# Hybrid attention and SSM layer: the input projection as seven half-size block products (Strassen), one product at a time

## Chip, cores and metric

The kernel runs on one core of a Trainium2 chip. The metric is the time of one execution in microseconds (us), measured on the device. The profile is of one execution, and all its rows are in us from the first instruction unless they say ns.

## What is computed

One layer over 2048 tokens of width 2048, all in float32. The input projection is the largest product: 2048 x 2048 by 2048 x 4608.

```python
h = rms_norm(x, norm_w)
proj = jnp.einsum('bld,de->ble', h, w_in)          # IN_W = 1024 + 256 + 256 + 1024 + 1024 + 1024
q, k, v, z_attn, u, z_ssm = jnp.split(proj, splits, axis=-1)
o_attn = swa_sink_attention(q, k, v, positions, q_norm_w, k_norm_w, sinks)   # window 128, 16 heads, 4 kv heads
o_attn = o_attn * jax.nn.silu(z_attn)
y = s5_ssm(u, a_re, a_im, log_step, b_re, b_im, c_re, c_im, d_skip)          # 64 groups of 16 channels
y = jax.nn.gelu(y)
y = y * jax.nn.sigmoid(y @ w_glu + b_glu)
o_ssm = y * jax.nn.silu(z_ssm)
merged = concat([rms_norm(o_attn, attn_out_norm_w), rms_norm(o_ssm, ssm_out_norm_w)])
out = x + jnp.einsum('ble,ed->bld', merged, w_out)
```

## The kernel before

Every large product is made of three passes in the fp32r type: each operand is split into a high part (a ScalarE cast) and a low part (a VectorE subtraction), and high x high, high x low and low x high are added up in PSUM.

**Tokens and panels.** The tokens are taken in two halves of 1024. For one half the whole normed and transposed x lies in SBUF, as 16 chunks of [128 features, 1024 tokens], each split into `xh` and `xl`. For the first half `x_first` (L242) loads rows of x, norms them and transposes them on TensorE; for the second half `x_stats` (L273) and `x_later` (L286) do so later, beside other work. The weight comes in units (`w_unit`, L304): a load of 256 KB, a cast `wh<-wr`, a subtraction `wl<-wr,wh`. A panel of u or z (`panel_feat`, L315) is 128 features by 1024 tokens: 16 chunks x 3 passes x 2 = 96 matmuls of 512 columns. A panel of q, k or v (`panel_tok`, L331) is 1024 tokens by 256 features with x as the weight operand: 16 x 8 x 3 = 384 matmuls of 256 columns. Over both halves there are 48 panels of the first kind and 12 of the second in the projection, 4608 matmuls of each kind.

**PSUM.** Four single banks (`psg`, [128, 512]) serve the panels, four more (`psa`) the small chains.

**What leaves a panel.** u, z, q, k and v go to DRAM scratch (`US`, `ZA`, `ZS`, `QS`, `KK`, `VS`). q and k are token-major: rotary and the norm of each head work along the free dimension (`rope_two`, L393), and `attend_in` (L467) transposes q on TensorE and splits it (`qst`).

**Order.** `run` (L1026) weaves panels with side work in steps (`weave`, L995): the SSM's tables (`ssm_setup`, L574) beside the first half's u, q, k, v and z; the first half's attention (`attend`, L503) beside the second half's start; the SSM itself (`ssm_pairs`, L784, 32 pairs) beside the rest of the projection. This stretch, up to about 1870 us, is called the front below. Then comes the tail: GLU of the first half (`glu`, L916) beside `tail_attn` (L885), the output projection of the first half (`out_panel`, L949) beside the second half's attention, GLU of the second half, and its output projection (`out_wide`, L970). The order of instructions within an engine is set by the tile framework, which schedules by a simulated timeline.

**Queues.** All loads and stores of tiles are issued from SyncE (SP), in one order. Staging tiles of 4 KB per partition come from one pool, `stg`, of 4 buffers; weight units from `wp` with 3 buffers each of raw, high and low.

```python
def tt(self, out, a, b, op, eng=None):      # nearly all two-input VectorE work is put down to this line, L84
    (eng or self.nc.vector).tensor_tensor(out=out, in0=a, in1=b, op=op)
```

## Time and profile before

| | |
|---|---|
| time, three runs | 2890.61 to 2895.2 us, median 2894.02 us |
| span of the profiled execution | 2892.7 us, the only time that it has |
| TensorE, matmuls | busy 2813.6 us (97%), 17123 instructions |
| TensorE, weight loads | 2515.5 us (87%) |
| VectorE | 1900.9 us (66%) |
| ScalarE | 968.2 us (33%) |
| GpSimd | 201.0 us (7%) |
| DMA | 369.09 MB, 128 GB/s over the span |

Busy time is the time in which an engine has at least one instruction under way; matmuls overlap one another, so that the duration of one is longer than the step from one to the next. VectorE's instructions overlap a little too. The span is the stretch from the first to the last instruction; it is 1.3 us under the median of the runs.

### The profile page before, as it was taken

What the parts mean: (1) busy time and instruction counts of PE and PEld (TensorE: products, weight loads), DVE (VectorE), ACT (ScalarE), POOL (GpSimd) and SP (SyncE); (2) the same over time, 40 slices, a digit from 0 to 9 for tenths busy, and PEclk for the clock granted to TensorE, in tenths of its full rate; (3) what the DMA queues carried; (4) which work ended last, traced back from release to release, by engine and by line L of the source; (5) the groups of instructions that cost most, each with busy time, mean ns of one, the idle gap of its engine ahead of it and who ended that gap; (6) DMA issues with size and microseconds to landing.
All of it is one profiled execution on the core that took longest, in us unless ns stands there. A gap on an engine that the chain in (4) does not pass through costs nothing.

```text
span 2892.7 us, 45678 instructions
## 1 busy us (share of the span) xinstructions
PE 2813.6 (97%) x17123; PEld 2515.5 (87%) x17123; DVE 1900.9 (66%) x4479; ACT 968.2 (33%) x2117; POOL 201.0 (7%) x341
## 2 busy tenths in 40 slices
PE   6899999989999999999999999998999999899999
PEld 5789999878888888888999988878999999778887
DVE  6681746856773776677779985378999875842222
ACT  6421212133442444333323332255444433521110
POOL 0000000001110021100000000000222220000000
PEclk9999999999999999999999999999999999999999
DMA  5842526553332533445455554343444436333321
GB/s 175 226 123 63 164 88 172 142 141 106 99 113 76 177 108 97 128 145 146 146 160 151 149 154 141 116 125 95 144 135 124 125 111 189 99 101 107 106 78 58
DMA packets 430541, 369.09 MB, mean 128 GB/s; under 512 B 56560, under 2 KB 388848, under 8 KB 430320
## 3 DMA queue, kind: packets, MB, share of 16 engines
q1 hardware_dynamic: 428256, 366.16, 42.6%
q8 instruction: 135, 2.21, 0.3%
q14 instruction: 86, 0.70, 0.1%
q10 hardware_dynamic: 2064, 0.01, 0.0%
HBM read 270.74 MB, written 99.55 MB: 128 GB/s over the span
## 4 chain that ended last, share of the span: by engine, by line
PE 81%; DVE 8%; DMA 7%; SPq 2%; ACT 1%; issue 1%; POOL 0%; ACTq 0%; POOLq 0%; DVEq 0%
PE psg L325 32%; PE psg L343 28%; PE psg L979 6%; PE pss L979 3%; DMA oa<-OA 2%; PE pss L516 2%; PE pso L556 2%; PE pso L979 1%; PE pst L979 1%; DVE ml L93 1%; DMA xst<-in_x_dram 1%; DVE yg L84 1%; PE pst L541 1%; DMA TCS<-St 1%; PE pss L810 1%
## 5 line engine op out<-in xcount | busy, mean ns | idle before, releaser
L84 DVE TENSOR_TENSOR wl<-wr,wh 128x512 fp32r<-128x512 f32 x456 | 315.4, 692 | 544.2 <-ACT wh L311 534.7
L311 ACT CAST wh<-wr 128x512 fp32r<-128x512 f32 x456 | 283.2, 622 | 1007.8 <-PE psg L325 330.9
L325 PE MATMUL psg<-xh,wl 128*128 128x512 f32 x1536 | 495.0, 394 | 7.2 <-DVE wl L84 7.2
L325 PE MATMUL psg<-xl,wh 128*128 128x512 f32 x1536 | 498.4, 395 | 0.0
L325 PE MATMUL psg<-xh,wh 128*128 128x512 f32 x1536 | 493.9, 395 | 0.5 <-ACT xh L235 0.5
L343 PE MATMUL psg<-wl,xh 128*128 128x256 f32 x1536 | 435.2, 284 | 0.0
L343 PE MATMUL psg<-wh,xh 128*128 128x256 f32 x1536 | 434.2, 284 | 1.0 <-ACT rx L389 1.0
L343 PE MATMUL psg<-wh,xl 128*128 128x256 f32 x1536 | 434.2, 284 | 0.0
L325 PEld LDWEIGHTS psg<-xh,wl 128*128 128x128 f32 x1536 | 287.8, 189 | 65.2 <-DVE wl L84 8.9
L325 PEld LDWEIGHTS psg<-xh,wh 128*128 128x128 f32 x1536 | 287.0, 189 | 57.2 <-ACT xh L235 0.9
L325 PEld LDWEIGHTS psg<-xl,wh 128*128 128x128 f32 x1536 | 288.1, 189 | 55.8
L343 PE MATMUL psg<-wh,mh 128*128 128x256 f32 x1024 | 289.9, 286 | 8.6 <-ACT tt L927 7.8
L343 PEld LDWEIGHTS psg<-wh,xh 128*128 128x128 f32 x1536 | 293.6, 192 | 1.4 <-ACT rx L389 1.2
L343 PEld LDWEIGHTS psg<-wl,xh 128*128 128x128 f32 x1536 | 294.2, 192 | 0.4 <-DVE wl L84 0.2
L343 PEld LDWEIGHTS psg<-wh,xl 128*128 128x128 f32 x1536 | 293.7, 192 | 0.0
L343 PE MATMUL psg<-wl,mh 128*128 128x256 f32 x1024 | 290.2, 285 | 0.6 <-DVE wl L84 0.6
L343 PE MATMUL psg<-wh,ml 128*128 128x256 f32 x1024 | 288.9, 285 | 0.0
L84 POOL TENSOR_TENSOR pm<-ph,sel 128x256 fp32r<-128x256 f32 x240 | 189.5, 811 | 983.1 <-ACT ph L544 647.2
L343 PEld LDWEIGHTS psg<-wh,mh 128*128 128x128 f32 x1024 | 195.1, 192 | 9.4 <-ACT tt L927 8.0
L343 PEld LDWEIGHTS psg<-wl,mh 128*128 128x128 f32 x1024 | 196.4, 192 | 0.8 <-DVE wl L84 0.8
L343 PEld LDWEIGHTS psg<-wh,ml 128*128 128x128 f32 x1024 | 195.4, 192 | 0.0
L533 ACT ACTIVATE sm<-pss,mx,rs 128x128 f32<-128x128 f32 x240 | 108.6, 459 | 96.3 <-DVE mx L93 90.5
(419 smaller groups left out, 4663.0 us busy)
## 6 DMA issues: line engine op xcount, KB each, us to landing
wr<-in_w_in_dram SPq DMA_DIRECT2D x296, 256.0 KB
wr<-in_w_out_dram SPq DMA_DIRECT2D x128, 256.0 KB
tb<-TCS SPq DMA_DIRECT2D x64, 256.0 KB
xr<-in_x_dram SPq DMA_DIRECT2D x64, 256.0 KB
out_dram<-xr SPq DMA_DIRECT2D x64, 256.0 KB
raw<-MBC SPq DMA_DIRECT2D x32, 384.0 KB
kst<-KK SPq DMA_DIRECT2D x56, 192.0 KB
xst<-in_x_dram SPq DMA_DIRECT2D x16, 512.0 KB
```

Of the source, the lines that this page charges most:

```text
L84: (eng or self.nc.vector).tensor_tensor(out=out, in0=a, in1=b, op=op)
L93: self.nc.vector.scalar_tensor_tensor(out=out, in0=a, scalar=s, in1=b, op0=op0, op1=op1)
L311: nc.scalar.copy(hi, raw)
L325: nc.tensor.matmul(ps[t], wt[:, kk, :], xx[k][:, t * 512:(t + 1) * 512], start=(k == 0 and i == 0), stop=(k == nkc - 1 and i == 2))
L343: nc.tensor.matmul(o, xx[k][:, sl], wt[:, kk, :], start=(k == 0 and i == 0 and t % 2 == 0), stop=(k == nkc - 1 and i == 2), skip_group_che ...
L516: nc.tensor.matmul(ps[:, h * 256:h * 256 + 256], qst[:, bq % 2, hp * 2 + h, :], kst[:, i, ksl], start=(h == 0 and i == 0), stop=(i == 1), ...
L533: nc.scalar.activation(sm[:, h, :], sc[:, h, :], AF.Exp, scale=rs[:, h:h + 1], bias=negm[:, h:h + 1], accum_out=den[:, h:h + 1])
L541: nc.tensor.transpose(pt[:, h * P:(h + 1) * P], sm[:, h, :], self.ident)
L556: nc.tensor.matmul(po, vst[:, blk + kb, :], pm[:, i, kb], start=(i == 0 and kb == 0), stop=(i == 1 and kb == 1))
L810: nc.tensor.matmul(o, m[:, g, 0:128], u[:, g, 384:640], start=(g == 0 and i == 0), stop=(i == 2), skip_group_check=True)
L979: nc.tensor.matmul(ps[t], xx[k0 + k][:, t * P:(t + 1) * P], wt[:, 0, :], start=(k == 0 and j == 0), stop=(k == 7 and j == 2))
```

## The change

The projection is computed for all 2048 tokens at once, as a 2 x 2 block product: tokens in halves, the 2048 inputs in halves, the output features in halves (paired as `fh` = 0, 1). Strassen's scheme in Winograd's form replaces the eight half-size products by seven. It is done in two groups: 10 pairs of panels (q, k, v, u) and 8 pairs (z_attn with z_ssm). In each group the products p = 0 to 6 run one after the other; a product is 10 or 8 panels, each of 8 chunks x 3 passes x 2 = 48 matmuls of 512 columns.

- **Left factors** (`form`, `place`). The host hands in x transposed as well (`xT`). The blocks and the four sums of blocks are formed once, 8 chunks of [128, 1024] each, stored to `AF` in DRAM, and loaded again for later products. x is still read row-wise for the norms (`x_stats`), and the factor of each token is spread over the partitions (`spread`, `rbc`).
- **Right factors** (`right`). The host lays the weight out as 4 KB runs per partition (`wl`). For p = 2, 5 and 6 the factor is a difference of two or three blocks, formed per panel; two of them are kept in `TW`.
- **Sums of products** (`gather`). Each panel's PSUM (a pair of banks, two such pairs) is added to a partial sum loaded from `CS` in DRAM, and the result is stored to `CS` or is an output.
- **q and k** are feature-major: `rope` works on [128 = 4 heads x 32, 1024 tokens] with both halves of each head; the first half to arrive waits in `RAW`. q is stored split (`QH`), so `attend_in` loads it ready with four DMAs, and k with four.
- z_attn is multiplied in `tail_attn` in place of `attend`.
- Staging: 7 buffers in the front and 4 in the tail; of x's split chunks 13 slots. The GLU weight is one load per panel (`wg`), the output weight comes in units of 512 KB.

```diff
-        self.wp = ep(tc.tile_pool(name="wp", bufs=3))
-        self.stg = ep(tc.tile_pool(name="stg", bufs=4))
-        self.gp = ep(tc.tile_pool(name="gp", bufs=4, space=PSUM))
+        self.gp = ep(tc.tile_pool(name="gp", bufs=2, space=PSUM))
...
+        return self.gp.tile([P, 1024], F32, tag="g", name="psg")
...
+    def norm_block(self, th, kh, k):
+        x = self.stage("xn")
+        r0 = kh * HT + k * P
+        self.ld.dma_start(x, self.a["xT"][r0:r0 + P, th * HT:(th + 1) * HT])
+        self.stt(x, x, self.nw[:, kh * 8 + k:kh * 8 + k + 1], self.rbc[th], ALU.mult, ALU.mult)
+        return x
...
+    def form(self, seq, k, first):
+        g = self.nc.gpsimd
+        p = seq % 7
+        st = lambda j, x: self.st.dma_start(self.AF[j, k], x)
+        if not first or p in (3, 4, 5, 6):
+            x = self.af_load(p, k)
+        elif p < 2:
+            x = self.norm_block(0, p, k)
+            st(p, x)
+        else:
+            n21 = self.norm_block(1, 0, k)
+            n22 = self.norm_block(1, 1, k)
+            st(6, n22)
+            s1 = self.stage("s1")
+            self.tt(s1, n21, n22, ALU.add)
+            st(3, s1)
+            x = self.af_load(0, k)
+            self.tt(n21, x, n21, ALU.subtract, g)
+            st(5, n21)
+            self.tt(x, s1, x, ALU.subtract)
+            st(2, x)
+            n12 = self.af_load(1, k)
+            self.tt(n12, n12, x, ALU.subtract, g)
+            st(4, n12)
+        return x
+
+    def place(self, seq, k, x):
+        slot = (8 * seq + k) % self.nslot
+        hi = self.xt.tile([P, HT], F32R, tag=f"xh{slot}", name=f"xh{slot}")
+        lo = self.xt.tile([P, HT], F32R, tag=f"xl{slot}", name=f"xl{slot}")
+        self.nc.scalar.copy(hi, x)
+        self.tt(lo, x, hi.bitcast(F32), ALU.subtract)
+        self.fac[seq % 2][k] = (hi, lo)
...
+        if p == 2:
+            b11, b12 = W(0, q1), W(0, q2)
+            self.tt(b12, b12, b11, ALU.subtract, g)
+            self.st.dma_start(self.TW[0, tw], b12)
+            b22 = W(1, q2)
+            self.tt(b22, b22, b12, ALU.subtract)
+            self.st.dma_start(self.TW[1, tw], b22)
+            return b22
+        if p == 3:
+            return self.w_load(self.TW[0, tw])
...
+        if p == 5:
+            b22, b12 = W(1, q2), W(0, q2)
+            self.tt(b22, b22, b12, ALU.subtract, g)
+            return b22
+        t2, b21 = self.w_load(self.TW[1, tw]), W(1, q1)
+        self.tt(t2, t2, b21, ALU.subtract, g)
+        return t2
+
+    def product(self, seq, group, first):
+        p = seq % 7
+        base, n = ((0, 10), (20, 8))[group]
+        free = self.nslot - 8
+        for i in range(n):
+            hi, lo = self.w_split(self.right(p, base + i, base + n + i))
+            ps = self.psg()
+            for k in range(8):
+                xh, xl = self.fac[seq % 2][k]
+                for j, (wt, xx) in enumerate(((hi, xh), (hi, xl), (lo, xh))):
+                    for t in range(2):
+                        nc.tensor.matmul(ps[:, t * 512:(t + 1) * 512], wt[:, k * P:(k + 1) * P], xx[:, t * 512:(t + 1) * 512],
+                                         start=(k == 0 and j == 0), stop=(k == 7 and j == 2))
+            if seq < 13 and i < free:
+                self.place(seq + 1, i, self.form(seq + 1, i, seq < 6))
+            if seq < 13 and i == n - 1:
+                for k in range(free, 8):
+                    self.place(seq + 1, k, self.form(seq + 1, k, seq < 6))
+            self.gather(p, group, i, ps)
+            yield
...
+        if p == 0:
+            t = self.stage("c0")
+            self.nc.scalar.copy(v(t), pv)
+            self.st.dma_start(cs(0), t)
+        elif p == 1:
+            done(0, 0, i, plus(load(0)))
+        elif p == 2:
+            self.st.dma_start(cs(1), plus(load(0)))
+        elif p == 3:
+            self.st.dma_start(cs(2), plus(load(1)))
+        elif p == 4:
+            done(0, 1, i, plus(load(2)))
+        elif p == 5:
+            b = load(1)
+            a = load(2)
+            self.st.dma_start(cs(3), plus(b))
+            done(1, 1, i, plus(a))
+        else:
+            done(1, 0, i, plus(load(3), ALU.subtract))
...
+            m, n = f2("rm"), f2("rn")
+            sh = (P, 2, 512)
+            self.stt(m, bc(a[:, s].unsqueeze(1), sh), wa, cs, ALU.mult, ALU.mult)
+            self.stt(n, bc(b[:, s].unsqueeze(1), sh), wb, cs, ALU.mult, ALU.mult)
+            self.tt(a[:, s], m[:, 0], n[:, 1], ALU.subtract)
+            self.tt(b[:, s], n[:, 0], m[:, 1], ALU.add)
...
+            self.x_stats(0)
+            for k in range(8):
+                self.place(0, k, self.form(0, k, True))
+            self.consts()
+            self.weave(pr(0, 2), self.setup_early(), 2, 0.0, 0.3, PU)
+        self.weave(pr(2, 5), self.ssm_setup(), 28, 0.0, 0.95, PU)
+        self.weave(pr(5, 14), self.mixers(), 65, 0.0, 1.0, PA)
+        phase.close()
```

## Rows read from the trace of the kernel before

**Rows 1.** The page, part 1: busy time, share and instructions of each engine.
```profile
PE 2813.6 (97%) x17123; PEld 2515.5 (87%) x17123; DVE 1900.9 (66%) x4479; ACT 968.2 (33%) x2117; POOL 201.0 (7%) x341
```

**Rows 2.** Tile yh: the first GLU matmul, that is the end of the front.
```profile
L325 PE MATMUL psg<-yh,wh x256: 387/389/632, 1870.3 to 2522.0; 128*128 128x512 f32 x128
```

**Rows 3.** Windows, front and tail: length, engines' busy us, granted clock, DMA share, GB/s.
```profile
0.00:1870.00 1870.00, 1822.52 (x10978) 1621.54 (x10979) 1260.98 (x3019) 619.94 (x1325) 99.60 (x213) 0.99 0.46 134
1870.00:2893.00 1023.00, 991.10 (x6147) 893.92 (x6145) 639.91 (x1460) 348.28 (x792) 101.36 (x128) 0.99 0.38 116
```

**Rows 4.** Groups of instructions on TensorE: one of three passes of each kind.
```profile
L325 PE MATMUL psg<-xh,wh 128*128 128x512 f32 x1536 | 493.9, 395 | 0.5 <-ACT xh L235 0.5
...
L343 PE MATMUL psg<-wh,xh 128*128 128x256 f32 x1536 | 434.2, 284 | 1.0 <-ACT rx L389 1.0
```

**Rows 5.** Chain that ended last: start, length, what; unbroken runs of matmuls.
```profile
1785.89 78.71 PE psg L325 x347
...
2373.85 52.56 PE psg L343 x438
```

**Rows 6.** SP's own waits: total us, times, longest.
```profile
SPq L308 <- DVE wl L84: 972.4, 288, 10.7
```

**Rows 7.** Timeline of TensorE: four transposes and the next matmul's start.
```profile
300.38 0.60 PE L733 MATMUL pst<-ident,BT 128*128 128x128 f32 x4
300.74 0.37 PE L343 MATMUL psg<-wh,xl 128*128 128x256 f32 x1
```

**Rows 8.** Timeline of VectorE: starts of neighbours in unbroken runs.
```profile
477.31 1.22 DVE L84 TENSOR_TENSOR tu<-St,us 128x1024 f32<-128x1024 f32 x1
478.45 1.22 DVE L84 TENSOR_TENSOR tv<-Ct,us 128x1024 f32<-128x1024 f32 x1
...
508.09 0.69 DVE L84 TENSOR_TENSOR tu<-St,us 128x512 f32<-128x512 f32 x1
508.69 0.69 DVE L84 TENSOR_TENSOR tv<-Ct,us 128x512 f32<-128x512 f32 x1
```

**Rows 9.** Groups of instructions on VectorE that the projection issues.
```profile
L84 DVE TENSOR_TENSOR wl<-wr,wh 128x512 fp32r<-128x512 f32 x456 | 315.4, 692 | 544.2 <-ACT wh L311 534.7 <-DMA wr<-in_w_in_dram 3.8 <-PE psg L325 2.5
...
L84 DVE TENSOR_TENSOR rtmp<-rx,rt 128x512 f32<-128x512 f32 x40 | 25.8, 686 | 0.0
```

**Rows 10.** Windows of three stretches: opening, end of GLU, output projection with attention.
```profile
0.00:100.00 100.00, 77.55 (x381) 63.29 (x382) 67.60 (x195) 56.64 (x97) 4.79 (x52) 1.00 0.58 178
...
1930.00:1985.00 55.00, 44.31 (x215) 37.80 (x214) 47.10 (x61) 32.95 (x42) 0.00 (x0) 0.88 0.25 79
...
1985.00:2373.00 388.00, 387.17 (x3261) 386.45 (x3260) 346.77 (x1054) 165.52 (x535) 101.36 (x128) 1.00 0.42 127
```

**Rows 11.** DMA issues: transfers and KB of each.
```profile
wr<-in_w_in_dram SPq DMA_DIRECT2D x296, 256.0 KB
...
xst<-in_x_dram SPq DMA_DIRECT2D x16, 512.0 KB
...
QS<-rx SPq DMA_DIRECT2D x16, 512.0 KB
```

**Rows 12.** Windows of 5 us with busy DMA engines, columns as in rows 3.
```profile
20.00:25.00 5.00, 1.11 (x4) 0.71 (x4) 4.38 (x22) 3.59 (x7) 0.00 (x0) 1.00 1.02 412
...
110.00:115.00 5.00, 4.65 (x21) 3.52 (x19) 5.00 (x9) 3.04 (x7) 0.00 (x0) 1.00 1.00 361
...
135.00:140.00 5.00, 4.74 (x21) 3.58 (x20) 4.83 (x33) 1.39 (x3) 0.00 (x0) 1.00 1.08 87
```

**Rows 13.** Tile pm, GpSimd and VectorE: duration ns min/median/max.
```profile
L84 POOL TENSOR_TENSOR pm<-ph,sel x240: 731/745/1248, 642.5 to 2367.7; 128x256 fp32r<-128x256 f32 x120
L84 DVE TENSOR_TENSOR pm<-pl,sel x240: 408/421/1021, 644.6 to 2368.0; 128x256 fp32r<-128x256 f32 x120
```

More of the change, by code (lines that the diff above doesn't have):

```diff
@@ new lines, in panel_glu @@
+    def panel_glu(self, m, xh, xl, evac):
+        nc = self.nc
+        ps = self.psg()
+        hi, lo = self.w_split(self.w_load(self.a["wg"][m]))
+        for k in range(8):
+            for i, (wt, xx) in enumerate(((hi, xh), (hi, xl), (lo, xh))):
+                for t in range(2):
+                    nc.tensor.matmul(ps[:, t * 512:(t + 1) * 512], wt[:, k * P:(k + 1) * P], xx[k][:, t * 512:(t + 1) * 512],
+                                     start=(k == 0 and i == 0), stop=(k == 7 and i == 2))
+        yield
+        for t in range(2):
+            evac(t, ps[:, t * 512:(t + 1) * 512])
@@ new lines, in run @@
+        with tc.tile_pool(name="rb", bufs=1) as pool:
+            self.rbc = [pool.tile([P, HT], F32, tag=f"rbc{h}", name=f"rbc{h}") for h in range(2)]
+            self.x_stats(0)
+            for k in range(8):
+                self.place(0, k, self.form(0, k, True))
[3 more added lines that the diff above has]
+        self.weave(pr(5, 14), self.mixers(), 65, 0.0, 1.0, PA)
@@ L1112, with laid_out @@
 _OUTS = [((1, 2048, 2048), "float32")]
+def laid_out(inputs):
+    o = {k: np.asarray(v) for k, v in inputs.items()}
+    o["xT"] = np.ascontiguousarray(o["x"][0].T)
+    half = lambda c0, two, i: [c0 + (i * 4 + h) * 64 + two * 32 + j for h in range(4) for j in range(32)]
+    run = lambda c0, m: list(range(c0 + m * P, c0 + m * P + P))
+    f = lambda two: ([half(C_Q, two, i) for i in range(4)] + [half(C_K, two, 0), run(C_V, two)]
+                     + [run(C_U, m + 4 * two) for m in range(4)])
+    panels = f(0) + f(1) + [run(C_ZA, m) for m in range(8)] + [run(C_ZS, m) for m in range(8)]
+    w = o["w_in"].reshape(2, 8, P, -1)
+    o["wl"] = np.ascontiguousarray(np.stack([w[:, :, :, c].transpose(0, 2, 1, 3).reshape(2, P, 1024) for c in panels], axis=1))
+    o["wg"] = np.ascontiguousarray(o["w_glu"].reshape(8, P, 8, P).transpose(2, 1, 0, 3).reshape(8, P, 1024))
+    q, k = o["q_norm_w"], o["k_norm_w"]
+    o["qk_gain"] = np.ascontiguousarray(np.stack([np.tile(v, 4) for v in (q[:32], q[32:], k[:32], k[32:])], axis=1))
+    return o
 def kernel(**inputs):
@@ L1123 @@
     arrays, args = {}, []
+    inputs = laid_out(inputs)
     for name in _INS:
```

500 lines of the change are left out of this document (221 added, 279 removed).

## Prediction

> **What bounds the kernel now.** I read the busy shares first [rows 1], to see which engine has no room: TensorE 97%, VectorE 66%. Then the span cut where the first GLU matmul starts [rows 2], because the change rewrites what lies before (the front) and hardly touches the tail. The front takes 1870 us, of which TensorE is busy 1822.5; VectorE is busy 1261 and the DMA engines move 134 GB/s at a share of 0.46 [rows 3]. So TensorE's queue of matmuls sets the front; the reader should see that two other resources have about a third and a half to spare, because the change spends exactly these. The list of groups [rows 4] shows the projection's two kinds of matmul. Their durations (395 and 284 ns) overlap, so prices come from the chain of waits, where unbroken runs give steps: 78.71 us / 347 = 0.227 us for 512 columns, 52.56 / 438 = 0.120 us for 256 [rows 5]. Of SP's own waits the longest total, 972 us, is the prefetch of weights waiting for a free buffer [rows 6]: today the transfers run ahead of the work.
>
> **TensorE's work.** Removed: 4608 x 0.227 + 4608 x 0.120 = 1045 + 553 = 1598 us. Put in: 7 products x 18 panels x 48 = 6048 matmuls of 512 columns, 1372 us. That is -226 us (more than an eighth would be 200, because 256-column matmuls cost more per column). Gone too are 256 transposes of x and, in the front, 64 of q; four in a row take 0.36 us [rows 7], so 320 x 0.09 = -29 us. The 32 transposes of k make room for 32 of v. New are some 150 small matmuls (head norms, spreading of the token factors): between 0.09 each, a transpose, and 0.28, a full unoverlapped duration [rows 4, 7], 14 to 43 us; I take 25. TensorE's busy time in the front becomes 1822 - 226 - 29 + 25 = 1592 us, and the old idle 48 us give way to new stalls, below.
>
> **VectorE's work in the front.** Neighbours start 1.14 us apart for 1024 elements and 0.60 for 512 [rows 8]. Removed: 288 weight subtractions at 0.60 (173 us) [rows 9]; scaling and splitting of x (66); half of q's splits and products with z (29); the old rotary and head norms of 20 half panels (24 us of rtmp [rows 9], 68 in 60 full-width operations, 29 in small ones: 121). Sum 389. Added at 1.14: 126 weight splits, 126 sums with PSUM (18 panels x 7; p = 0 is ScalarE's, p = 5 has two), 112 splits of left factors, 32 normings, 16 block sums, 18 weight differences: 430, or 490 us. Plus rotary: per q panel four double multiplies, four half-width sums, two splits and some dozen small ones, 10.4 us x 8; per k panel about 25 us x 2, for the reciprocal root runs over 512 columns there: 133. Net +234, so 1495 us against TensorE's 1592. ScalarE stays far below both (620 now [rows 3]). VectorE at 89% (347 of 388) cost TensorE nothing in the stage of attention beside the output projection [rows 10], so equal loads need not stall, but little slack is left.
>
> **Transfers in the front.** Before: 1870 us x 134 GB/s = 251 MB [rows 3]. Removed: weights 296 x 0.262 MB, x 48 x 0.524, q scratch 12.6, z for attention 4.2, rotary tables 7.3: 127 MB [rows 11], with the counts of the code. Added, counted in the code in transfers of 0.524 MB: weights 18 x 13 = 234, left factors 192, x for the norms 32, partial sums 18 x 11 = 198, waiting q and k 20, split q and k 32 more than before, rotary tables 20, q loads 16: 744, or 390 MB. Together 514 MB. Long runs reach 361 to 412 GB/s for 5 us, tables of short runs 87 [rows 12]. 514 MB at 361 is 1424 us: on average hidden, but not in every product.
>
> **New stalls, in order.**
> 1. Opening. Nothing can be normed before all of a half's rows (8.4 MB) are read: 20 us at 412 GB/s, 47 at the 178 that the first 100 us show [rows 10, 12]; I take 22. With latency, the reciprocal root, the spreading and the first chunk, the first product starts near 40 us. Each of its first 8 chunks needs two VectorE passes, 2.3 us, so the first panel takes 18 us instead of 10.9. +48.
> 2. Product 1 forms the sums for product 2: per chunk 4 loads and 5 stores, 37.7 MB, plus weights, partial sums and outputs 16.5 MB. 54 MB at 361 GB/s is 150 us against 109 of matmuls: +41 (0 if part of it is drawn into product 0; 77 at the 291 GB/s that 134 at a share of 0.46 makes).
> 3. p = 2 moves 3 weight loads, 2 stores, 2 transfers of partial sums and a left factor per panel: 4.6 MB with the tables beside it, 12.7 us against 10.9; +18 in the first group, +8 in the second.
> 4. Rotary. In p = 4 and p = 6 the first five panels each bring one. Adding up how long each staging tile lives, I get about 85 us of buffer per q panel and 157 per k panel; by 7 buffers 12 and 22 us against 10.9. The next panel's partial sum needs a buffer of the same pool before PSUM can be emptied, and its load stands behind the others in SP's one queue. Between 0 (VectorE alone could follow) and 60 per half if nothing overlaps; I take 25 each: +50.
> 5. VectorE near its limit from p = 5 on, where attention and SSM run beside: +30, between 0 (its 89% above cost nothing) and 130 (third rival).
>
> Sum +195; front 1592 + 195 = 1787 us.
>
> **Tail.** 1023 us [rows 3]. Attention loses 64 transposes, -6. The products with z come to tail_attn, 16 x 1.14 = 18 us, half of it counted, since at the end of GLU VectorE is busy 47 of 55 us [rows 10] and sets the pace: +9. Today the last z panel (some 22 us of matmuls) covers the loads and splits before the first GLU matmul; in the change the last SSM pair, its store and reload stand bare: 0 to 25, I take +14. Tail 1040.
>
> 1787 + 1040 = 2827 us of span; the median stands 1 us above the span: **2828 us**, 2.3% below 2894. Its own range, from the bounds of stalls 1 to 5, is 2760 to 2885.
>
> **Rivals.**
> A, everything hides. Only TensorE's work and the opening stay: 1592 + 48 + 1032 = 2672 us. For it: today's transfers wait for buffers, not the other way round [rows 6]. Against it: the 7 staging buffers serve every new stream, and product 1 asks for 54 MB in 109 us. 18%.
> B, slower: one queue of transfers becomes the bound. The front needs 514 MB / 1787 us = 288 GB/s as a mean over almost two milliseconds, twice today's 134. If the queue, in order and with few buffers, keeps to 93% of the 291 GB/s that today's mix makes at a full share, the front is 514 / 271 = 1897 us, with 24 for the reading of rows ahead of the first product 1921, and the time 2962 us. It decides from a front of 2892.7 - 1040 = 1853 us, that is from a mean of 514 / (1853 - 24) = 281 GB/s downwards: then the change is slower. For it: at 5 us the rows show such rates, over 100 us only 178 [rows 10, 12]. Against it: the new transfers are runs of 4 KB, whose rows stand at 361 and above. 30%.
> C, GpSimd holds VectorE up. The change gives 70 subtractions of 1024 elements to GpSimd. Its 128x256 ones take 731 ns at least, so about 2.9 us each (no less than VectorE's 1.14). VectorE's operation of the same form beside it has a median of 421 ns but a longest of 1021 [rows 13]: some wait. If all 70 hold it, VectorE's front is 1495 + 203 = 1698 us, at 95% busy 1787, with the opening 1835: about 2880 us. 15%.
>
> The Trainium skill, SBUF — State Buffer, "Who interferes with whom", says that GpSimd and a VectorE instruction with two SBUF inputs exclude each other for a whole instruction. That is rival C at its full 203 us; the median of 421 ns shows that most VectorE instructions of before met no such lock, so the trace bears the rule out only for a part of them.
>
> **Chances.** Forecast 37% (nearly all of it faster), A 18% faster, B 30% (28 slower, 2 within), C 15% (7 faster, 4 within, 4 slower). A measurement of this kernel can tell 0.2% (6 us) from no change. Faster 0.60, within 0.08, slower 0.32. The range that leaves out about a tenth on either side cuts A near its middle and B at its far end: 2690 to 2980. Cases of both signs hold most of the chance; the forecast's own range stands above.
>
> **What would show it.** Right: 6048 matmuls of 512 columns at a step of 0.227 us and no 256-column ones before GLU; the first GLU matmul near 1787 us; idle TensorE before about 45 us, in product 1 (some 165 to 315 us) and where q and k turn; DMA near 290 GB/s over the front, VectorE over 80% busy there. Where TensorE idles the granted clock should dip, as it does to 0.88 in [rows 10] where 11 of 55 us were idle; that is not priced apart. Wrong: stalls spread evenly over all products with the DMA share at 0.9 (B); VectorE without gaps and its two-input operations of 1024 elements well above 1.22 us (C); PSUM pairs that wait for partial sums in every product, which would make the second pair of banks, not the transfers, the cause.

## Result

The changed kernel takes 3203.45 us (median of four runs, 3195.96 to 3207.84), the kernel before 2892.97 beside it: a ratio of 1.107 [1.1053, 1.1087]. It is slower by 310 us, where 2828 us and faster were forecast. The profiled execution has a span of 3199.1 us. (One run below, e13_rt, had a mean granted clock of 0.75, and 0.75 also from 120 to 160 us, where TensorE had no pause; its times are left aside, and the same kernel stands in the table as e13_rt_again.)

The page of the changed kernel, part 1, answers to [rows 1]:
```profile
PE 2728.8 (85%) x13883; PEld 2295.6 (72%) x13883; DVE 2189.6 (68%) x4078; ACT 953.4 (30%) x1803; POOL 409.7 (13%) x416
```
TensorE has less to do than before, and is idle for 470 us where it was idle for 79. The first GLU matmul, tile `yh`, answers to [rows 2]:
```profile
L454 PE MATMUL psg<-yh,wh x256: 387/393/763, 2138.0 to 2817.4; 128*128 128x512 f32 x128
```
The front has grown from 1870 to 2138 us, +268; the tail from 1023 to 1061. The windows of the changed kernel answer to [rows 3], columns as there: front, tail, then five stretches of the front (product 1, product 4, product 6, the second group, and what follows the last panel).
```profile
0.00:2138.00 2138.00, 1725.10 (x7803) 1403.65 (x7804) 1550.98 (x2728) 628.15 (x1121) 301.25 (x288) 0.89 0.73 242
2138.00:3199.00 1061.00, 1003.70 (x6080) 891.99 (x6080) 638.62 (x1351) 325.25 (x682) 108.50 (x128) 0.98 0.39 118
177.00:363.00 186.00, 134.73 (x536) 105.50 (x534) 103.46 (x179) 21.34 (x25) 49.73 (x23) 0.85 0.94 327
627.00:865.00 238.00, 148.34 (x680) 119.97 (x679) 191.06 (x422) 50.84 (x90) 13.03 (x15) 0.80 0.69 213
1001.00:1207.00 206.00, 161.94 (x753) 132.15 (x752) 177.28 (x363) 67.95 (x155) 39.54 (x34) 0.84 0.67 220
1207.00:1924.00 717.00, 704.49 (x3315) 581.67 (x3313) 565.25 (x885) 263.49 (x465) 120.55 (x102) 0.99 0.72 246
1924.00:2138.00 214.00, 70.94 (x241) 55.36 (x242) 151.39 (x226) 51.70 (x85) 1.33 (x13) 0.50 0.39 118
```
Three things are to be seen. The amounts of work in the front (VectorE 1551 us; 242 GB/s, that is 517 MB) are near those forecast (1495 us, 514 MB). Products 4 and 6, which turn q and k, take 238 and 206 us where ten panels' matmuls need some 110, with neither VectorE (191 and 177 us) nor the DMA engines (0.69 and 0.67) full. And after the last panel come 214 us in which TensorE has 71 us of work at the lower clock (0.50 of full speed, 1.2 GHz): the rest of the SSM's pairs, with nothing beside them (14 of the 32 had their state still to come).

Where attention begins, tile `kst`, the first score matmul, first of the kernel before and then of the changed one:
```profile
L516 PE MATMUL pss<-kst,qst x512: 274/281/365, 616.5 to 2346.1; 128*128 128x256 f32 x171
```
```profile
L602 PE MATMUL pss<-kst,qst x512: 274/282/562, 831.6 to 2588.2; 128*128 128x256 f32 x171
```
Before, q, k and v of the first half were complete at 617 us; now each head's second half comes in product 4. Attention begins 215 us later, and from there to the first GLU matmul it is 1306 us against 1254. 215 + 52 make up the whole of the 268.

The products' ends, by the last sum of each in VectorE's timeline, against those that the prediction's terms give (157, then 150, 127, 109, 134, 109, 134, then the rest):

| stretch | forecast, us | measured, us |
|---|---|---|
| to the end of product 0 | 157 | 177.5 |
| product 1 | 150 | 186 |
| products 2 and 3 | 236 | 263 |
| product 4 | 134 | 238 |
| product 5 | 109 | 137 |
| product 6 | 134 | 205 |
| second group and side work, to GLU (forecast: what remains) | 867 | 932 |
| front | 1787 | 2138 |

The front was 351 us longer than forecast. Cut at the last panel's sum (1924 us), 137 us of this lie before it, as longer products, and 214 us behind it, as pairs beside which no panel runs.

### The profile page after: what moved, and what is told of

It reads as the page before. It is cut to its first block, busy times and chain, and to the rows that moved or that the text cites. A ratio compares the mean times of both kernels' runs of the same rounds, so it can differ in the third digit from the quotient of the medians.

```text
span 3199.1 us, 39115 instructions
## 1 busy us (share of the span) xinstructions
PE 2728.8 (85%) x13883; PEld 2295.6 (72%) x13883; DVE 2189.6 (68%) x4078; ACT 953.4 (30%) x1803; POOL 409.7 (13%) x416
## 5 line engine op out<-in xcount | busy, mean ns | idle before, releaser
L382 PE MATMUL psg<-xh,wh 128*128 128x512 f32 x2016 | 662.0, 408 | 112.6 <-DVE cs L87 68.0
L382 PE MATMUL psg<-xh,wl 128*128 128x512 f32 x2016 | 654.5, 404 | 12.0 <-DVE wl L87 12.0
L382 PE MATMUL psg<-xl,wh 128*128 128x512 f32 x2016 | 656.2, 404 | 7.5 <-DVE xl L87 7.5
L382 PEld LDWEIGHTS psg<-xh,wh 128*128 128x128 f32 x2016 | 388.4, 195 | 204.5 <-issue 66.6
L87 DVE TENSOR_TENSOR wl<-wr,wh 128x1024 fp32r<-128x1024 f32 x206 | 270.9, 1315 | 379.0 <-ACT wh L325 357.1
L382 PEld LDWEIGHTS psg<-xh,wl 128*128 128x128 f32 x2016 | 385.9, 193 | 100.1 <-DVE wl L87 14.8
L382 PEld LDWEIGHTS psg<-xl,wh 128*128 128x128 f32 x2016 | 388.2, 194 | 96.2 <-DVE xl L87 8.9
L325 ACT CAST wh<-wr 128x1024 fp32r<-128x1024 f32 x206 | 215.7, 1048 | 779.7 <-PE psg L382 286.1
L473 PE MATMUL psg<-wh,mh 128*128 128x256 f32 x1024 | 292.4, 287 | 20.4 <-ACT tt L1018 14.4
L87 DVE TENSOR_TENSOR cs<-cs,psg 128x1024 f32<-128x1024 f32 x126 | 151.9, 1215 | 101.9 <-PE psg L382 93.0
L87 POOL TENSOR_TENSOR wr<-wr 128x1024 f32<-128x1024 f32 x54 | 137.2, 2541 | 498.0 <-DMA wr<-in_wl_dram 357.4
L87 DVE TENSOR_TENSOR pm<-pl,sel 128x256 fp32r<-128x256 f32 x240 | 149.8, 664 | 35.6 <-PE pso L642 33.0
L87 DVE TENSOR_TENSOR xl<-af,xh 128x1024 fp32r<-128x1024 f32 x96 | 121.8, 1274 | 18.8 <-ACT xh L312 18.2
L1073 PE MATMUL psg<-wh,mh 128*128 128x512 f32 x256 | 101.6, 397 | 7.0 <-ACT tt L1018 7.0
```

What stands on the lines that cost most here:

```text
L325: self.nc.scalar.copy(hi, raw)
L382: nc.tensor.matmul(ps[:, t * 512:(t + 1) * 512], wt[:, k * P:(k + 1) * P], xx[:, t * 512:(t + 1) * 512], start=(k == 0 and j == 0), stop=( ...
L473: nc.tensor.matmul(o, xx[k][:, sl], wt[:, kk, :], start=(k == 0 and i == 0 and t % 2 == 0), stop=(k == nkc - 1 and i == 2), skip_group_che ...
L1073: nc.tensor.matmul(ps[t], xx[k0 + k][:, t * P:(t + 1) * P], wt[:, 0, :], start=(k == 0 and j == 0), stop=(k == 7 and j == 2))
```

## Experiments

Each is the changed kernel with one edit, if nothing else is said. The last three columns: products 4 and 6 of the first group (last sum to last sum), the first score matmul of attention, and the first GLU matmul.

| run | time, us | p = 4, p = 6 | first score | first GLU |
|---|---|---|---|---|
| changed kernel | 3203 | 238, 205 | 832 | 2138 |
| e1_no_side | 3694 | 181, 185 | | 2632 |
| e2_no_rope | 2995 | 127, 132 | 746 | 1934 |
| e3_mix_early | 3180 | 238, 242 | 826 | 2114 |
| e4_dve_subs | 3177 | 247, 207 | 826 | 2110 |
| e5_sum_bufs | 3167 | 187, 183 | 843 | 2102 |
| e6_stores_act | 3184 | 245, 209 | 834 | 2134 |
| e7_defer | 3216 | 117, 153 | 942 | 2147 |
| e8_pair_bufs | 3218 | 244, 209 | 834 | 2152 |
| e9_wide_stage | 3710 | 175, 181 | | 2650 |
| e10_pair_lo | 3147 | 240, 206 | 825 | 2088 |
| e11_order | 3194 | 245, 202 | 887 | 2134 |
| e12_combo | 3104 | 178, 189 | 835 | 2041 |
| e13_rt_again | 3168 | 188, 195 | 855 | 2106 |
| e14_combo_rt | 3084 | 175, 176 | 818 | 2017 |
| e16_rt_no_side | 3662 | 159, 159 | | 2590 |
| e17_interleave | 3112 | 234, 212 | 833 | 2048 |
| e18_all | 3076 | 180, 211 | 828 | 2009 |

These are single runs, so only differences of some 10 us and more are read. The expectations count 192 us for product 6 and 431 for both, where the stretch runs from the last sum but one of product 5 to the last but one of product 6; from last sum to last sum, as in this table, it is 205 and 443. None comes near the 2893 of the kernel before.

**The products alone.**
```diff
-        self.weave(pr(2, 5), self.ssm_setup(), 28, 0.0, 0.95, PU)
-        self.weave(pr(5, 14), self.mixers(), 65, 0.0, 1.0, PA)
+        self.weave(pr(2, 14))
+        for _ in self.ssm_setup():
+            pass
+        for _ in self.mixers():
+            pass
```


> Same work in another order: the seven products run with nothing woven beside products 2 to 13, then the SSM's tables, then attention and the SSM, alone. Theory V (VectorE's in-order queue carries tables, rotary and sums in one product, and TensorE waits for the sums): the first five panels of p = 4, 183 us in the changed kernel, fall to about 85 (some 14 us of VectorE per q panel, 29 for k), those of p = 6 likewise, and the last panel's sum comes near 1550 us (now 1924). Rival T (transfers and staging buffers hold the products up by themselves): those panels stay above 30 us each, the panels of the second group stay near 12.8 us, and the last sum comes after 1700 us. The whole is longer in both cases, near 3600 us, since the SSM's 32 pairs run at about 14.4 us each uncovered.

The products end at 1694 us. Windows of this run: products 1 and 4, the second group, then first-half attention alone and the 32 pairs alone.
```profile
178.00:356.00 178.00, 133.71 (x537) 104.72 (x535) 94.38 (x83) 22.50 (x23) 51.77 (x24) 0.88 0.99 343
579.00:760.00 181.00, 138.15 (x620) 112.15 (x619) 107.67 (x163) 39.48 (x48) 11.67 (x4) 0.87 0.61 211
...
1060.00:1695.00 635.00, 628.83 (x2707) 507.78 (x2706) 286.05 (x330) 147.79 (x156) 64.82 (x25) 0.99 0.64 222
1899.00:2170.00 271.00, 159.70 (x625) 130.43 (x624) 248.29 (x829) 123.71 (x456) 97.66 (x116) 0.53 0.30 87
2170.00:2632.00 462.00, 166.62 (x566) 129.83 (x566) 331.61 (x501) 109.29 (x188) 3.14 (x31) 0.50 0.34 99
```
Neither expectation was met: the first five rotary panels of product 4 take 132 us (183 in the changed kernel; 85 expected under theory V, over 30 each under T). The second group's 56 panels run with TensorE full, nearly all 11.2 us apart, at 222 GB/s: transfers as such don't hold the products up, and rival B falls as a rule for the whole front. In product 1 it holds: the DMA engines are busy at a share of 0.99 for 178 us. Product 4 is the new case: 181 us, VectorE at 108, DMA at 0.61, and still 43 us without a matmul. And 1694 us for the products alone, opening included, is more than the 1598 us of matmuls that the whole projection was before: opening and stalls inside the products eat Strassen's saving without any help from side work.

**Rotary left out** (with head norms and tables; q and k are split and stored as they come).

> Leaves the rotary embedding, the head norms and their table loads out: q and k are only split and stored. Theory V: p = 4 falls from 238 to about 150 us and p = 6 from 192 to about 140, some 130 us sooner at the end of p = 6, most of it seen in the whole. Rival T: the 10.5 MB of tables are 2% of the transfers, and all stores and the waiting halves stay, so p = 4 stays above 200 us and the whole within 50 us of the changed kernel.

-208 us, the largest single effect, and more than either expectation had; products 4 and 6 fall to 127 and 132. Attention begins 85 us sooner (746), the last panel's sum comes 204 us sooner (1720), and the pairs behind it still take 214 us. From the first score to GLU it is 1188 us instead of 1306: the side work's length depends on the panels beside it.

**What makes a rotary panel long.** The staging pool first:
```diff
-            t = self.stage("cs")
+            t = self.cg.tile([P, HT], F32, tag="g", name="cg")      # a pool of its own, 2 buffers; x slots 13 -> 12
```


> The partial sums that gather loads get two staging buffers of their own, and x's split chunks 12 slots instead of 13 (the memory for it). Nothing is left out. Theory L (a rope panel is long because the next panel's partial sum waits for one of the 7 staging buffers that rotary holds): products 4 and 6 of the first group, 238 + 192 us in the changed kernel, take below 330 together, and the time falls by 70 to 130 us, to 3070 to 3130. Rival P (the ropes themselves are the chain: VectorE's passes, the one queue of transfers and the head-norm matmuls in TensorE's own order): they stay above 400 together, and the time within 30 us of 3203.

Products 4 and 6 fell by 73 together, but product 5, with two sums per panel, rose from 137 to 179; time -36. At 370 us they lie between the two theories. Product 1 fell to 118 us, but product 2 rose from 136 to 184: the 57 us that end product 1 in the changed kernel are gone, 82 us stand at the start of product 2, and the two together take 302 us instead of 321. e12_combo and e14_combo_rt, which also have this pool, show the same (some 295).
```diff
+        self.stg = wide.enter_context(tc.tile_pool(name="stg", bufs=15))     # in e1_no_side, for the products only
```


> As e1_no_side (all products first, the side work after them; nothing left out), but with 15 staging buffers instead of 7 while the products run. To be compared with e1_no_side (3694 us; its products 1, 4 and 6 of the first group took 178, 181 and 185 us to the last sum, and the products ended at 1694). Theory L (rotary panels are long because 7 staging buffers hold too little): products 4 and 6 fall to 130 or less each, the products end near 1590, time near 3590. Rival P (the rope's own chain from engine to engine, and the sum queued behind it on VectorE): they stay above 160 each. Product 1 had its DMA engines busy at a share of 0.99: if transfers bound it, it stays within 8 us of 178.

With twice the buffers products 4 and 6 stand at 175 and 181 (181 and 185): where the products run alone, the number of buffers is not the cause, and the half of the prediction's step 4 that counts buffers falls for them. (Beside side work it is not excluded: e5_sum_bufs took 73 us off.) Product 1 fell from 178 to 162 us, more than the 8 us allowed, so buffers had a part there. Product 0 ended at 161 us instead of 179, so they had one in the opening too. Window of product 1:
```profile
161.00:323.00 162.00, 130.51 (x528) 103.29 (x526) 84.49 (x64) 19.82 (x21) 48.75 (x19) 0.91 0.98 360
```
```diff
-        self.st = self.nc.sync
+        self.st = self.nc.scalar
```


> All stores are issued from ScalarE's queue instead of SyncE's; loads stay on SyncE's. Nothing is left out. If loads wait behind stores in the one queue, products 4 and 6 of the first group fall by over 80 us together and the wait at the end of product 1 (57 us) by half: time 3050 to 3120. If the buffers are what they wait for, these stretches move by less than 40 us; and where ScalarE now waits in order for VectorE's results before it can issue a store, its casts come later, so that the time may rise by up to 50 us.

Products 4 and 6 grew by 11, the wait at the end of product 1 stayed at 57: loads were not waiting behind stores.
```diff
-            hi, lo = self.w_split(self.right(p, base + i, base + n + i))
+            m = (5, 4, 6, 0, 7, 1, 8, 2, 9, 3)[i] if group == 0 else i
+            hi, lo = self.w_split(self.right(p, base + m, base + n + m))
...
-            self.gather(p, group, i, ps)
+            self.gather(p, group, m, ps)
```


> Only the order of the first group's ten panels is changed in each product: v, k, u, q, u, q, u, q, u, q instead of four q, k, v, four u. Nothing is left out. If a rope delays the panels because five of them follow each other (more work on VectorE and in staging than two pairs of PSUM banks bridge), every second panel without one gives time, and products 4 and 6 fall from 431 to below 350 together, the time by 60 to 110. If each rope stalls the next sum by its own chain, wherever it stands (as deferred ropes did in e7_defer, 26 to 43 us for the panel beside each), they stay above 400.

447 us for both, no less than 443: a rope stalls the next sum wherever it stands. What it waits for is in the traces. In e9_wide_stage, VectorE: two sums of product 4 and the rotary multiplications between them,
```profile
600.18 1.21 DVE L87 TENSOR_TENSOR cs<-cs,psg 128x1024 f32<-128x1024 f32 x1
...
608.27 1.28 DVE L96 SCALAR_TENSOR_TENSOR rm<-rw,gain,cs 128x1024 f32<-128x1024 f32 x1
...
615.70 1.28 DVE L96 SCALAR_TENSOR_TENSOR rm<-rw,gain,cs 128x1024 f32<-128x1024 f32 x1 [3.62 <-DMA cs<-RT]
...
624.97 1.21 DVE L87 TENSOR_TENSOR cs<-cs,psg 128x1024 f32<-128x1024 f32 x1
```
and SyncE's issues in the same stretch:
```profile
600.11 0.53 SPq L508 DMA_DIRECT2D cs<-RT  x1
608.38 0.34 SPq L319 DMA_DIRECT2D wr<-in_wl_dram  x1
608.81 0.53 SPq L508 DMA_DIRECT2D cs<-RT  x1
```
The table load goes out at 608.81, right behind a weight load at 608.38, which needs a raw weight buffer that `wl<-wr,wh` (607.13) gives back; that split needs the weight buffer of the panel that TensorE has just left. So the load starts late, the multiplication waits for it, and the next sum stands behind the multiplications in VectorE's order: 24.8 us from sum to sum. The tables were therefore kept in SBUF:
```diff
-            cs = f2("cs")
-            self.ld.dma_start(cs, self.RT.rearrange("r j a t -> (r j) a t")[:, :, t0:t0 + 512])
+            cs = self.rt[:, :, s]                 # loaded once per half, ahead of products 4 and 6; 12 slots for x
```


> e1_no_side (3694 us, all products first) with the resident rotary tables of e13_rt, 12 slots for x, and the 7 staging buffers as they were. Nothing is left out. Theory Q: products 4 and 6 fall from 181 and 185 us to 140 or less each, the products end near 1610 and the time near 3610. If the rope's chain of engines is long by itself: above 165 each.

159 and 159 instead of 181 and 185: part of it, not all (140 was expected). The q panels came from 17 to 29 us down to 15 to 20, the panel of k stayed at 39 to 45. Timeline of VectorE there, the sum of k, the second read of its norm, the sum of v:
```profile
661.74 1.22 DVE L87 TENSOR_TENSOR cs<-cs,psg 128x1024 f32<-128x1024 f32 x1
...
677.49 0.69 DVE L93 TENSOR_SCALAR ms<-pso 128x512 f32<-128x512 f32 x1
...
706.44 1.22 DVE L87 TENSOR_TENSOR cs<-cs,psg 128x1024 f32<-128x1024 f32 x1 [3.97 <-DMA cs<-CS]
```
Between 669.5 and 702.5 VectorE is never idle for more than 0.6 us: the reciprocal root over 512 columns, twice, and the products with it. For k it is mostly VectorE's own work, put ahead of v's sum, and v's transposes wait in TensorE's order (20.3 us in that stretch). What ends last is a transfer even so: from 702.5 to 706.44 VectorE waits for the partial sum of v. SyncE issued that load at 700.71, behind two weight loads of which the second had waited until 700.29 for GpSimd's subtraction:
```profile
700.71 0.39 SPq L404 DMA_DIRECT2D cs<-CS  x1
```

In the changed kernel itself the same edit, e13_rt and again:

> The rotary tables of one half of the tokens (8 KB per partition) are loaded once, ahead of products 4 and 6 of the first group, and stay, in place of two loads per rope; x's split chunks have 12 slots instead of 13 for it. Nothing is left out. Theory Q (the rope waits for its tables, whose loads stand in SyncE's order behind weight loads that wait for a buffer, and the next panel's sum stands behind the rope on VectorE): products 4 and 6 fall from 431 to below 340 together and the time by 60 to 120. If VectorE's own work (191 of 238 us in product 4) sets the pace: above 390, time within 40.

> The kernel of e13_rt once more. With e16_rt_no_side (products 4 and 6 at 159 us each instead of 181 and 185) theory Q now gives: products 4 and 6 at 370 to 400 together instead of 431; the time falls by less than that, 10 to 40 us, since attention and pairs follow as one chain. If VectorE's work alone sets rotary panels: above 420.

188 + 195 = 383, -35 us: within the second expectation, but not the first, which had asked for less than 340. Product 5 gave some of it back (168 us instead of 137). Last, the ropes as side steps:
```diff
+        yield from self.ropes(0)              # in mixers, ahead of attention; ropes(1) between the pairs
```


> Rotary is taken out of the panels: both halves of each head are stored as they come, and the ten ropes run as side steps, five ahead of the first half's attention (beside product 5 on), five between the SSM's pairs in the second group. Nothing is left out. Theory L (rope stalls TensorE only because the next panel's sum needs what rope holds, and its own work fits beside other panels): products 4 and 6 take 120 to 140 each, and the time falls by 80 to 180 us, to 3020 to 3120 (208 is what leaving rotary out gave). Rival V (VectorE's work is what counts, wherever it stands): the ropes' some 13 us of VectorE each come back as later pairs, products 4 and 6 fall but the rest of the SSM after the last panel grows by as much, and the time stays within 40 us.

Products 4 and 6 fell by 173 us together, and the time rose by 12. The panels beside a rope took 26 to 43 us in product 5 instead, attention began 110 us later, and GLU came 9 us later. The run doesn't separate two readings: the ropes now lengthen the chain of side work ahead of attention, and they take VectorE from the panels wherever they stand (rival V, whose 40 us it stays within).

**The chain of side work.** In every kernel of the table that weaves, from 1181 to 1317 us lie between the first score matmul and the first GLU matmul (1254 before). Alone the same work takes 735 us (e1_no_side, from 1896 to 2632).
```diff
-        self.weave(pr(5, 14), self.mixers(), 65, 0.0, 1.0, PA)
+        self.weave(pr(5, 14), self.mixers(), 65, 0.0, 0.7, PA)
```


> Attention and SSM steps are handed out over the first 70% of the last nine products instead of all of them. Theory L (the SSM's chain comes too late and its last 15 pairs run uncovered): the stretch between the last panel and the first GLU matmul, 216 us, falls under 110, and the whole falls by 80 to 120 us. Rival (a pair beside panels takes 25 us because engines and transfers are full there, so that the panels lose what the pairs gain): the whole stays within 30 us.

-24 us. The first pair began 73 us sooner (1412 instead of 1485), but a pair took some 25 us beside panels, as in the changed kernel (some 18 in the kernel before), and the panels ended 33 us later. So what the rival says is seen as well: panels and side work take time from each other. Alone a pair takes 14.4; timeline of VectorE among the pairs of e1_no_side, the low parts `lo` and the state `H`:
```profile
2174.01 1.82 DVE L87 TENSOR_TENSOR lo<-raw,hi 128x512 fp32r<-128x512 f32 x3 [2.17 <-PE pst L928]
2184.07 0.75 DVE L96 SCALAR_TENSOR_TENSOR H<-B,sgn,A 128x510 f32<-128x510 f32 x1
2188.43 1.82 DVE L87 TENSOR_TENSOR lo<-raw,hi 128x512 fp32r<-128x512 f32 x3 [2.17 <-PE pso L928]
2198.49 0.75 DVE L96 SCALAR_TENSOR_TENSOR H<-B,sgn,A 128x510 f32<-128x510 f32 x1
```
`lo` of a pair waits for the last matmuls (L928) of the pair before. The change had cut `lo`, `raw` and `tb` from two buffers to one, which the prediction does not price (`H` had one before, too).
```diff
-                tb = pool.tile([P, 2, 2, 256], F32, tag="tb", name="tb", bufs=1)
+                tb = pool.tile([P, 2, 2, 256], F32, tag="tb", name="tb")         # and raw; setup's loads from ScalarE's queue
```


> Two edits in separate stretches, nothing left out: (a) the loads of the SSM's setup are issued from ScalarE's queue instead of SyncE's, (b) the SSM pairs' inputs and tables have two buffers each instead of one. (a) If the last three sums of product 1 wait behind these loads of short runs, its last gap falls from 57 us to 25 or less (three sums at 7 us each by transfer), time -30; if it is the transfers' own, it stays above 45. (b) If a pair beside panels takes 25 us because its loads wait for the pair before, it comes to 18 us as in the kernel before, some 21 pairs are done at the last panel instead of 17, and the rest after it falls from 216 to about 130, time -80; if VectorE or the order of priorities sets the pace, the rest stays above 180.

Both parts missed: the last gap of product 1 grew to 74 us, the pairs stayed at 22 to 31. Not the inputs, then; next `lo`, and with it what had one buffer before the change:
```diff
-                lo = pool.tile([P, 2, 640], F32R, tag="lo", name="lo", bufs=1)
+                lo = pool.tile([P, 2, 640], F32R, tag="lo", name="lo")           # H, Hh, Hl and y likewise
```


> The changed kernel with two buffers instead of one for the SSM pair's low parts (lo), for H, Hh, Hl and the y that shares H's; the raw inputs and tables stay at one. Nothing is left out. Theory S (a pair takes 24 us beside panels because the next pair's first product needs lo, which the last product of the pair before still reads, so that only one pair is under way): pairs come every 17 to 19 us beside panels and under 11 us after them, 10 or fewer are left at the last panel instead of 15, the rest after it falls from 216 to under 110, and the time by 90 to 150 us, to 3050 to 3110. Rival V (the engines' queues, shared with the panels, set the 24 us; or the transfers of raw): pairs stay above 22 us and the time within 30 us.

-56 us: pairs 18 to 28 us apart instead of 20 to 31, so that 11 instead of 14 are left at the last panel, and 160 us after it instead of 214. The direction of theory S, about half its size; after the last panel pairs come 13.9 us apart instead of 14.4, where it had under 11, so `lo` does not set that pace. Whether `lo` or `H` gave the gain beside panels was not separated, and what else keeps a pair at over 18 us there is not settled. Then the order of the chain:
```diff
-            yield from self.attend_all(pool, 0)
-        yield from self.ssm_pairs()
+            for _ in range(16):                    # half of attention, then a pair and a step in turn
+                next(att)
+                yield
+            for _ in self.ssm_pairs():
+                yield
+                if next(att, 1) is None:
+                    yield
```


> The second 16 of the first half's 32 attention steps alternate with the first 16 of the SSM's pairs instead of preceding all of them; for the memory attention has one buffer each of its inputs and outputs in the front, x's split chunks 12 slots, raw weights 3 buffers. Nothing is left out. Theory C (attention and pairs are one chain of side work, 555 us and then 32 pairs, that starts when product 4 has completed q, k and v, and its length sets the front's end): the pairs begin near 1240 instead of 1485, 5 or fewer are left at the last panel, and the first GLU matmul comes near 2000 instead of 2138: time 3050 to 3100. Rival E (the engines' work sets it; the order of side work changes nothing): within 40 us of 3203.

-91 us, although the panels ended later than in the changed kernel (last sum at 1960 instead of 1924). The first pair's `H` came at 1214 instead of 1485, and 88 us of pairs are left behind the last panel instead of 214. Tiles `H` and `yh`, first of the changed kernel and then of this run (`yh` of the changed kernel stands above):
```profile
L96 DVE SCALAR_TENSOR_TENSOR H<-B,sgn,A x32: 735/749/2789, 1484.6 to 2122.6; 128x510 f32<-128x510 f32 x32
```
```profile
L96 DVE SCALAR_TENSOR_TENSOR H<-B,sgn,A x32: 730/746/2742, 1213.6 to 2033.3; 128x510 f32<-128x510 f32 x32
L454 PE MATMUL psg<-yh,wh x256: 387/393/766, 2048.4 to 2730.9; 128*128 128x512 f32 x128
```
So it is the chain of side work, not the last panel, that ends the front, and its order counts (rival E had at most 40 us). The expected 3050 to 3100 was missed by 12 us, for pairs beside attention took 21 to 44 us.

**GpSimd's subtractions on VectorE.**
```diff
-        g = self.nc.gpsimd
+        g = self.nc.vector
```


> The 70 subtractions of 1024 elements that GpSimd does go to VectorE. Third rival of the prediction (GpSimd locks VectorE out for whole instructions): the 70 x 2.5 us of blocking go and 70 x 1.14 us come, the whole falls by 50 us or more. Theory V: VectorE has 80 us more in its queue, the whole is unchanged to 60 us slower.

-27 us, between the two expectations. VectorE's busy time with 70 more operations is 2186.1 us, 3.5 less than in the changed kernel; at 1.14 each they are 80 us, so by this estimate holding by GpSimd had cost some 83, 1.2 us per subtraction. Page part 1 of that run:
```profile
PE 2721.0 (86%) x13883; PEld 2294.4 (72%) x13883; DVE 2186.1 (69%) x4148; ACT 952.0 (30%) x1803; POOL 235.6 (7%) x346
```

**Several together.** e12_combo joins e5, e11, e4, e10 and earlier SSM tables (`0.95` to `0.65`), so that they don't fall on the ropes; e14_combo_rt adds the resident rotary tables; e18_all joins e17, e11, e4, the earlier tables and the resident ones.

> Together: two own buffers for the partial sums with 12 slots for x (product 5's short-lived second sum from the common pool), the panel order of e11_order, GpSimd's 70 subtractions on VectorE, the pairs' low parts and H with two buffers, and the SSM's tables ended at 65% of products 2 to 4 so that they are done before the ropes. Nothing is left out. If the single causes add up: pairs -120, panel order and tables -100, own buffers -20, subtractions -27: 2940 (2890 to 3000). If the ropes conserve their cost, 3030 to 3080.

> e12_combo (3104 us) with the resident rotary tables of e13_rt and 11 slots for x. Nothing is left out. Theory Q: products 4 and 6 (178 and 189 us there) come to 130 to 150 each and the time to 3010 to 3060. If VectorE's work sets the pace: within 30 of 3104. With 11 slots five chunks of the next factor are formed at the end of a product, which may cost product 1 up to 35.

> e17_interleave with the panel order of e11, GpSimd's 70 subtractions on VectorE, the tables ended at 65% of products 2 to 4, and the resident rotary tables (11 slots for x). Nothing is left out. If the causes add up: e17's gain and some 100 us of shorter products 2, 4 and 6: 2940 to 3000. It is faster than the kernel before only if the pairs then take no more than 18 us beside panels, which I don't expect.

3104, 3084 and 3076 us: all short of what adding up would give, and e12_combo also of the worse case expected (3080). e14_combo_rt took 15 us off the two products of e12_combo and 24 off the front. No run joins the order of e17_interleave with the buffers of e10_pair_lo. From the first score to GLU it is 1205, 1199 and 1181 us in the three.

## Why the prediction was wrong

**The step that failed first** is the sum "front 1592 + 195 = 1787": it takes the front's end to be TensorE's work plus TensorE's stalls, so that the front ends with the last panel. In the changed kernel the last panel's sum comes 137 us after that end, and 214 us of pairs follow it, where the prediction had allowed 0 to 25 for one bare pair. e17_interleave shows that the end belongs to the side work: with the pairs begun 271 us sooner the front is 90 us shorter, although its panels end 37 us later.

This side work cannot start before the first half's q, k and v are complete. The prediction's own terms put the end of product 4 at 157 + 150 + 127 + 109 + 134 = 677 us; attention begins some 30 us before it (832 against 864 in the changed kernel), and before it was 1254 us from there to GLU. 646 + 1254 + 1040 = 2940 us would have been the sum by that length, and slower. This is hindsight, and partly luck: in the kernel before, TensorE was busy for 1251 of these 1254 us, so they are the length of the side work beside full panels and not its own (735 alone). That it came out at 1181 to 1317 in all woven runs is shown. What stretches it is shown only in part, by e10_pair_lo (buffers), e17_interleave (order) and e2_no_rope (rotary beside it); the rest is open, and e18_all is still some 180 us behind the kernel before.

**Term 4, rotary +50**, was mis-sized. Products 4 and 6 came out at 129 and 96 us above 109 each, not 25; alone (e1_no_side) at 72 and 76. The mechanism was half right: a sum waits behind the rope, and loads stand behind others in SP's one queue. But "by 7 buffers 12 and 22 us" was not what it waits for with the products alone (e9_wide_stage); it is the table load that goes out late, k's reciprocal root on VectorE, and, woven, the SSM's tables, which are the only side work beside product 4 (238 us instead of 181, VectorE 191). What is left of a q rope's 15 to 20 us with resident tables was not taken apart.

**Terms 1 to 3.** Opening: product 0 ended 20 us late, of which 15 staging buffers take away 18 (e9_wide_stage against e1_no_side); the term names no buffers. Product 1: +77 instead of +41, the forecast's own upper bound; the DMA engines were at 0.94 to 0.99. Its 57 us at the end are the last three of eight formings, which take 17 us each alone as well. Products 2 and 3: 27 us over.

**Term 5, VectorE +30**, did not come where it was put: from the end of product 6 to the last panel TensorE is idle for 12 of 717 us. Whether VectorE's load there delays the pairs instead was not tested.

**The range.** The bounds given with terms 1, 2, 4 and 5 add up to 231 us above the sum, that is 3059 and not 2885. The measured time is beyond both.

**TensorE's work** was forecast at 1592 us and is busy for 1725. The matmul counts were right (L382: 3 x 2016 = 6048):
```profile
L382 PE MATMUL psg<-xh,wh 128*128 128x512 f32 x2016 | 662.0, 408 | 112.6 <-DVE cs L87 68.0 <-ACT xh L312 16.2 <-DVE rry L96 15.9
```
408 ns against 395 in [rows 4]: in the stretches with stalls the granted clock is 0.80 to 0.85, so that a stall costs again in the matmuls after it. By the trace, 229 of the 6048 matmuls take over 0.5 us and start 0.425 us apart, which makes some 45 us (an estimate); the prediction named this and priced it at nothing. A step of 0.2325 us instead of 0.227 (last section) makes another 33. The 71 us under the bare pairs are at the lower clock too.

**Right** were VectorE's work (1551 for 1495, with some 83 of holding by GpSimd in it), the transfers (517 MB for 514), the second group's panels without side work (11.2 us) and nearly the tail (1061 + 2 outside the span, for 1040 + 1).

**Rivals.** A fell with the products alone at 1694 us, where it had 1640 for the whole front. B has the sign, not the mechanism: a DMA share of 0.94 to 0.99 is seen in product 1 (0.91 in product 2), one of 0.61 to 0.86 in the stretches read behind them. C is real and small: -27 us in e4_dve_subs, 83 us of VectorE's time instead of 203, with a median of 2.41 us per subtraction instead of 2.9.

## What to carry to other kernels

When a change delays a result that side work needs, add up the side work from there to its end, as well as the engine that seems full; the trace of before has its length beside the panels, from first to last, though not what sets it. A reformulation that saves an eighth of the matmuls pays only while everything around each panel fits beside the shorter panel: here the products took 1694 us by themselves, opening and stalls included, where the matmuls they replace took 1598. When memory is tight, look first at which buffers the change has cut to one, and who then waits for whom.

## What was not expected of the hardware

**GpSimd holds VectorE for nearly a whole instruction.** Timeline of the changed kernel, GpSimd's subtraction and two of VectorE's beside it:
```profile
380.06 2.88 POOL L87 TENSOR_TENSOR wr<-wr 128x1024 f32<-128x1024 f32 x1 [14.59 <-DVE PR L87]
380.64 2.39 DVE L87 TENSOR_TENSOR rd<-PI,lr 128x64 f32<-128x64 f32 x1
382.95 1.21 DVE L87 TENSOR_TENSOR wl<-wr,wh 128x1024 fp32r<-128x1024 f32 x1
```
The operation at 380.64 takes 0.27 us elsewhere (379.18 in the same timeline); here it ends within 0.1 us of GpSimd's. In [rows 13] the median hid this. The rule of the Trainium skill, SBUF — State Buffer, "Who interferes with whom" (an exclusive lock for a whole instruction), agrees with these rows. The price per subtraction was 1.2 us here by the estimate above, less than the 2.41 us that one takes.

**Transfers mostly of 4 KB runs hold their rate**: 343 GB/s over 178 us (e1_no_side) and 360 over 162 (e9_wide_stage) in product 1, where the rows of before showed 361 for 5 us only.

**Two lengths of the matmul step at the full clock.** Windows of 10 us in product 0 of the changed kernel (TensorE alone, matmuls begun), and of e2_no_rope:
```profile
140.00:150.00 10.00, 10.00 (x44) 1.00 0.31 106
```
```profile
140.00:150.00 10.00, 10.00 (x46) 1.00 0.31 106
```
A panel takes 11.15 us there and 10.9 here, as it would by the step of [rows 5]; over 126 panels some 30 us. All other variants of the table stand at 11.1 to 11.2. Why is open, and with one profiled execution of each it is not shown that the program makes the difference.
